# Samples' local attention over all 128 rows: both heads' scores in one matmul, padded values

## The chip, the cores and the metric

One Trainium2 chip, of which the program uses one core. The metric is the device time of one execution in microseconds. The engines are named as in the profile: PE (matrix products), PEld (its weight loads), DVE, ACT, POOL and SP; each works off its own list of instructions in order, and DMAs are issued from SP, ACT and POOL.

## The reference

One step of a streaming encoder of two layers: 512 prompt frames and 8 samples of 16 new frames each, model width 2048. Each layer projects the normalised input with `w_in`, splits the result among three groups (a causal convolution, a sliding-window attention with 16 query heads of 64 over 2 key heads, an attention over 256 memory tokens), gates them, and adds an output projection with `w_out` to the residual. The change touches the window attention of the samples: each sample's 16 frames read 128 cached keys and its own 16.

```python
def swa_sample(q, k, v, cache_k, cache_v, sinks, bias):
    qh = q.reshape(B, S, 2, 8, 64)                   # key heads, queries per key head, width
    kf = jnp.concatenate([cache_k, k], axis=1)       # 128 + 16 keys
    vf = jnp.concatenate([cache_v, v], axis=1)
    o = sink_attention(qh, kf, vf, bias, None, sinks)
    ...
def sink_attention(q, k, v, bias, mask, sinks):
    s = jnp.einsum('...ikgd,...jkd->...kgij', q, k).astype(jnp.float32) * SWA_SCALE + bias
    ...
    p = jnp.exp(s - m)
    w = p / (jnp.sum(p, axis=-1, keepdims=True) + jnp.exp(sink - m))
    return jnp.einsum('...kgij,...jkd->...ikgd', w, v)
```

## The kernel before

Activations are held with channels on the 128 partitions and 640 frames (512 + 8 x 16) in the free dimension. A layer runs 46 projections of `w_in`, each 4 x 4 x 3 x 2 matmuls over 320 columns (`proj`, L749): weights and activations are split in a high and a low part (`wh`, `wl`; `split`, L138 on ACT and L139 on DVE) and three of the four products are taken. Between these matmuls stand those of the attention groups. Their values are plain f32, whose matmul leaves two records in the profile.

The order on each engine is the scheduler's: it places the instructions by a timeline of its own, with priorities, and `issue_after` adds an order between two instructions. Attention work is written as generators with one `yield` between scores and values; `push` starts the next one's first half and then finishes the last one's second half. The samples' generators, `swa_sample(l, b0, held)` for `b0` = 0, 2, 4, 6, are pushed after the last `q` projection and after the following one. Each handles two samples; they are called pairs 1 to 4 in the following.

On the partitions, rows 0 to 63 belong to key head 0 and rows 64 to 127 to key head 1: of the queries `qs` (128 columns a sample: 8 queries by 16 frames) as of the keys `kc` (144 columns a sample: 128 cached, 16 new). The two heads' scores are two matmuls that contract 64 rows each (L571). DVE adds the bias and takes the maximum (L574), ACT takes the exponential (L587), DVE normalises (L600). PE transposes the weights, 128 and 16 columns apart (L603, L604), ACT copies both out of PSUM (L606, L607), and two matmuls into the same sum contract 128 cached values (L608) and 16 new ones (L609).

Of tiles: `kc` has one buffer, `g2` (values, weights, copies, also of the prompt's attention and of the pointwise weights) eight, PSUM's `a` four. POOL loads `kc` (L555) and copies the new keys in (L556), once for pairs 1 and 2 and once for pairs 3 and 4; it also loads the cached values (L558), the new frames' values from a scratch in DRAM (L560), the pointwise weights of the convolution group (L470, used at L477) and the samples' memory keys (L672). Before the samples come the prompt's generators (`swa_prompt`, transposes L528 and L531, values L540), and behind all projections the splits of the gated result into `HL` and its combinations, on DVE and ACT, and the output projection (L749 and L810). L203 sums squares or values over partitions with a matrix of ones, in f32.

Of the kernel before, what the change touches and what calls it, by code (L numbers as in the profile page):

```python
# [12 lines left out]
AF = mybir.ActivationFunctionType  # L13
# [3 lines left out]
P = 128  # L17
# [7 lines left out]
ST = 16  # L25
# [33 lines left out]
def build(nc, tc, ctx, A):  # L59
# [23 lines left out]
    def tl(shape, tag, bufs, dt=F32, pl=None):  # L83
        uid[0] += 1
        pl = pl or (cur[home[tag]] if tag in home else sb)
        return pl.tile(shape, dt, tag=tag, name=f"{tag}_{uid[0]}", bufs=bufs)
# [7 lines left out]
    def g2(shape, dt=F32):  # L94
        return tl(shape, "g2", 8, dt)
# [10 lines left out]
    def pa():  # L106
        return tl([P, 512], "a", 4, F32, ap_)
# [4 lines left out]
    ve, ac, gp, pe, sy = nc.vector, nc.scalar, nc.gpsimd, nc.tensor, nc.sync  # L112
# [6 lines left out]
    ident = sb.tile([P, P], F32, tag="ident", name="ident")  # L119
# [125 lines left out]
    def lsm(l, base, n=1):  # L245
        o = l * SM_L + base
        return sm[:, o:o + n]
# [301 lines left out]

    def swa_sample(l, b0, held):  # L550
        sk = lsm(l, SM_SS, 2)
        if b0 % 4 == 0:
            kc = tl([P, 576], "kc", 1).rearrange("p (b n) -> p b n", b=4)
            with tc.issue_after(late):
                gp.dma_start(kc[:, :, :P], A["ckT"][l, b0:b0 + 4].rearrange("b p n -> p b n"))  # L555
            gp.tensor_copy(kc[:, :, P:], ks[:, b0 * ST:(b0 + 4) * ST].rearrange("p (b n) -> p b n", b=4))  # L556
            vb = g2([P, 4, P])
            gp.dma_start(vb, A["cv"][l, b0:b0 + 4].rearrange("b p n -> p b n"))  # L558
            vn = g2([ST, 4, P])
            gp.dma_start(vn, vscr[l, b0 * ST:(b0 + 4) * ST, :].rearrange("(b i) d -> i b d", i=ST))  # L560
            held[:] = [kc, vb, vn]
        kc, vb, vn = held
        mx, ng, es, sm_, rd = (sml([P, 2, 2]) for _ in range(5))
        xs = []
        for bb in range(2):
            b = b0 + bb
            ps = pa().rearrange("p (j n) -> p j n", j=2)
            x = g2([P, 2, 144])
            for h in range(2):
                rows = slice(h * 64, (h + 1) * 64)  # L570
                pe.matmul(  # L571
                    ps[:, h, :144], qs[rows, b * P:(b + 1) * P], kc[rows, b % 4, :], start=True, stop=True
                )
                ve.tensor_tensor_reduce(  # L574
                    out=x[:, h, :], in0=ps[:, h, :144], in1=bias_s[:, h, :], scale=1.0, scalar=-3.0e38,
                    op0=ALU.add, op1=ALU.max, accum_out=mx[:, bb, h:h + 1],
                )
            xs.append(x)
        skb = sk.unsqueeze(1).to_broadcast([P, 2, 2])
        ve.tensor_tensor(out=ng, in0=mx, in1=skb, op=ALU.max)  # L580
        ve.tensor_scalar(out=ng, in0=ng, scalar1=-1.0, scalar2=None, op0=ALU.mult)
        ve.tensor_tensor(out=es, in0=ng, in1=skb, op=ALU.add)
        ac.activation(es, es, AF.Exp)
        for bb in range(2):
            x = xs[bb]
            for h in range(2):
                ac.activation(  # L587
                    x[:, h, :], x[:, h, :], AF.Exp, bias=ng[:, bb, h:h + 1], accum_out=sm_[:, bb, h:h + 1]
                )
        ve.tensor_tensor(out=es, in0=es, in1=sm_, op=ALU.add)  # L590
        ve.reciprocal(rd, es)
        yield
        pss = [pa(), pa()]
        po = pa().rearrange("p (j n) -> p j n", j=2)
        for bb in range(2):
            x = xs[bb]
            b = b0 + bb
            ps = pss[bb]
            for h in range(2):
                ve.tensor_scalar(  # L600
                    out=x[:, h, :], in0=x[:, h, :], scalar1=rd[:, bb, h:h + 1], scalar2=None, op0=ALU.mult
                )
                pe.transpose(ps[:, h * P:(h + 1) * P], x[:, h, :P], ident)  # L603
                pe.transpose(ps[:ST, 256 + h * P:256 + (h + 1) * P], x[:, h, P:], ident)  # L604
            pt = g2([P, 512])
            ac.activation(pt[:, :256], ps[:, :256], AF.Copy)  # L606
            ac.activation(pt[:ST, 256:], ps[:ST, 256:], AF.Copy)  # L607
            pe.matmul(po[:, bb, :], vb[:, b % 4, :], pt[:, :256], start=True, stop=False)  # L608
            pe.matmul(po[:, bb, :], vn[:ST, b % 4, :], pt[:ST, 256:], start=False, stop=True)  # L609
        for bb in range(2):  # L610
            s, b4 = divmod(b0 + bb, 4)
            for h in range(2):
                rows = slice(h * 64, (h + 1) * 64)
                o = s * HT + PT_ + b4 * ST
                y = R[rows, B0:B0 + 8, o:o + ST]
                ve.tensor_tensor(
                    out=y, in0=po[rows, bb, h * P:(h + 1) * P].rearrange("p (t i) -> p t i", i=ST), in1=y,
                    op=ALU.mult,
                )
# [669 lines left out]
```

## Time and profile before

| | |
|---|---|
| median of 3 runs | 1848.38 us (1848.2 to 1850.27) |
| the profiled execution | 1848.52 us |
| its span, first to last instruction | 1846.7 us |
| mean granted clock of PE | 0.997 |
| PE, PEld busy | 1817.5 us, 1766.3 us |
| DVE, ACT, POOL busy | 1257.8 us, 786.6 us, 160.7 us |
| score matmuls L571 | 64 records, mean 318 ns |
| value matmuls L608, L609 | 32 records each, mean 379 and 426 ns |
| transposes L603, L604 | 32 records each, mean 290 and 272 ns |

An engine's busy time is the union of its instructions' lengths; matmuls are pipelined, so a record's length is longer than what it adds to the engine's time, which shows in the distance from one start to the next. In a timeline row stand the start, the length, engine, line, operation, tiles (written <- read), shape and count of merged records, and in brackets the idle time ahead with what ended it.

### The profile page before, as it was taken

Reading aid. Unit: us, or ns where it says so; the run is one execution under the profiler, and the core shown is the slowest. Engines: PE = TensorE matmul, PEld = TensorE weight load, DVE = VectorE, ACT = ScalarE, POOL = GpSimd, SP = SyncE. Lnnn points to the kernel's source line nnn. Section 1 sums busy time; section 2 is a strip of 40 time slices with the busy share of each in tenths; the row PEclk is TensorE's granted clock in tenths of the full one; section 3 lists DMA queues with packets and bytes.
Section 4 is the critical chain, followed back from the end, with each engine's and each line's share of the span. In section 5 each row is a group of like instructions: output and inputs, shape, how many; then the busy total and the mean of one; then the engine's idle time right before and its main releaser. Section 6 shows DMA issues by size and latency. Waiting matters only on the chain.

```text
span 1846.7 us, 32347 instructions
## 1 busy us (share of the span) xinstructions
PE 1817.5 (98%) x12612; PEld 1766.3 (96%) x12612; DVE 1257.8 (68%) x2562; ACT 786.6 (43%) x1609; POOL 160.7 (9%) x351
## 2 busy tenths in 40 slices
PE   8999999999999999999999999999999999999996
PEld 7999999999998999999999999999999899989996
DVE  7959989567555435966686999766655444676765
ACT  7832224556544334533352222555755333533331
POOL 1121210000000010100020000000000010010000
PEclk9999999999999999999999999999999999999998
DMA  8844442222222343543333332222232244452233
GB/s 281 294 122 107 103 127 76 74 63 72 84 81 76 92 158 117 167 135 112 111 98 92 81 86 77 74 68 76 67 87 81 75 132 132 140 175 76 77 113 120
DMA packets 89001, 202.30 MB, mean 110 GB/s; under 512 B 11872, under 2 KB 16912, under 8 KB 88816
## 3 DMA queue, kind: packets, MB, share of 16 engines
q1 hardware_dynamic: 68848, 139.75, 25.3%
q0 software_dynamic: 17536, 57.60, 10.1%
q10 hardware_dynamic: 2464, 2.88, 0.4%
q8 instruction: 99, 1.62, 0.4%
q14 instruction: 54, 0.44, 0.1%
HBM read 184.84 MB, written 20.33 MB: 111 GB/s over the span
## 4 chain that ended last, share of the span: by engine, by line
PE 94%; DVE 3%; DMA 1%; issue 0%; ACT 0%; DVEq 0%; ACTq 0%
PE z L749 59%; PE a L810 9%; PE z L810 9%; PE z L301 2%; PE a L278 2%; PE a L497 2%; PE a L540 2%; PE a L477 2%; PE z L1134 1%; DVE R L1167 1%; PE a L528 1%; DMA wr<-w_in 1%; PE a L636 1%; PE a L675 1%; PE a L662 1%; PE a L571 1%
## 5 line engine op out<-in xcount | busy, mean ns | idle before, releaser
L749 PE MATMUL z<-HL,wh 128*128 128x320 f32 x4992 | 973.8, 312 | 0.0
L749 PEld LDWEIGHTS z<-HL,wh 128*128 128x128 f32 x4992 | 787.8, 188 | 8.9 <-issue 5.6
L749 PE MATMUL z<-HL,wl 128*128 128x320 f32 x2496 | 584.1, 312 | 1.0 <-DVE wl L139 1.0
L749 PEld LDWEIGHTS z<-HL,wl 128*128 128x128 f32 x2496 | 419.6, 188 | 4.5 <-issue 1.6
L138 ACT ACTIVATE wh<-wr 128x512 fp32r<-128x512 f32 x316 | 198.6, 629 | 467.4 <-PE z L749 383.9
L139 DVE TENSOR_TENSOR wl<-wr,wh 128x512 fp32r<-128x512 f32 x316 | 217.7, 689 | 177.8 <-ACT wh L138 165.4
L425 DVE SCALAR_TENSOR_TENSOR R<-R,sm 128x128 f32<-128x128 f32 (+1 forms) x480 | 235.2, 550 | 0.1
L138 ACT ACTIVATE sh<-sr 128x768 fp32r<-128x768 f32 (+1 forms) x125 | 98.2, 788 | 203.3 <-PE z L810 92.4
L810 PE MATMUL z<-HL,sh 128*128 128x320 f32 x728 | 161.1, 309 | 2.9 <-ACT sh L138 2.9
L139 DVE TENSOR_TENSOR sl<-sr,sh 128x768 fp32r<-128x768 f32 (+1 forms) x125 | 110.0, 882 | 38.7 <-ACT sh L138 38.5
L810 PEld LDWEIGHTS z<-HL,sh 128*128 128x128 f32 x728 | 121.6, 188 | 4.0 <-ACT sh L138 4.0
L810 PE MATMUL z<-HL,sl 128*128 128x320 f32 x364 | 113.6, 312 | 2.3 <-DVE sl L139 2.1
L810 PEld LDWEIGHTS z<-HL,sl 128*128 128x128 f32 x364 | 68.3, 188 | 4.9 <-DVE sl L139 4.9
L810 PE MATMUL a<-th,sh 128*128 128x320 f32 x234 | 72.2, 308 | 0.0
L810 PE MATMUL a<-th,sl 128*128 128x320 f32 x234 | 72.2, 308 | 0.0
L810 PE MATMUL a<-tl,sh 128*128 128x320 f32 x234 | 72.2, 308 | 0.0
L810 PE MATMUL a<-HL,sh 128*128 128x320 f32 x312 | 68.9, 308 | 0.0
L139 DVE TENSOR_TENSOR g<-a,g 128x512 fp32r<-128x512 f32 x80 | 49.6, 634 | 27.1 <-ACT g L138 26.5
L501 DVE CUSTOM_DVE_ANT_0 g<-a,R 128x256 f32<-128x256 f32 (+1 forms) x128 | 46.4, 388 | 23.4 <-PE a L497 20.0
L138 ACT ACTIVATE g<-a 128x512 fp32r<-128x512 f32 x80 | 42.2, 552 | 42.3 <-PE a L531 29.9
L513 ACT ACTIVATE g<-g,sml 128x256 f32<-128x256 f32 (+1 forms) x128 | 59.7, 468 | 0.0
L816 DVE TENSOR_TENSOR R<-a,R 128x320 f32<-128x320 f32 x78 | 37.1, 489 | 25.3 <-PE a L810 24.8
(262 smaller groups left out, 2512.0 us busy)
## 6 DMA issues: line engine op xcount, KB each, us to landing
wr<-w_in SPq DMA_DIRECT2D x304, 256.0 KB, 2.7
sr<-w_out SPq DMA_DIRECT2D x52, 384.0 KB, 3.2
sr<-w_out SPq DMA_DIRECT2D x34, 256.0 KB, 2.6
u<-w_mv SPq DMA_DIRECT2D x16, 512.0 KB, 3.8
u<-cmkT POOLq DMA_DIRECT2D x16, 512.0 KB, 4.3
u<-cmv POOLq DMA_DIRECT2D x16, 512.0 KB, 4.4
u<-w_mk SPq DMA_DIRECT2D x14, 512.0 KB, 4.4
R<-xT SPq DMA_DIRECT2D x16, 320.0 KB, 4.1
```

The source lines that it names most:

```text
L138: a = ac.activation(hi, raw, AF.Copy)
L139: v = ve.tensor_tensor(out=lo, in0=raw, in1=hi.bitcast(F32), op=ALU.subtract)
L278: pe.matmul(ps[ct][:, :256], w[:, ws], mslot(l, k, lo), start=k == 0 and n == 0, stop=k == NK - 1 and n == 2,)
L301: pe.matmul(psv[:, m, :], mslot(l, k, lo)[:, ms], w, start=k == 0 and n == 0, stop=k == NK - 1 and n == 2,)
L425: ve.scalar_tensor_tensor(out=o, in0=x, scalar=w, in1=o, op0=ALU.mult, op1=ALU.add)
L477: pe.matmul(ps[:, :HT], w[:, ws], x[:, k, :], start=n == 0, stop=n == 11)
L497: pe.matmul(ps[:, j, c0:256], q[:, p * P:(p + 1) * P], kk[n][h][:, (p - 1) * P + c0:(p + 1) * P], start=n == 0, stop=n == 1,)
L501: ve.tensor_tensor_reduce(out=x[:, j, c0:], in0=ps[:, j, c0:], in1=bt[:, c0:], scale=1.0, scalar=-3.0e38, op0=ALU.add, op1=ALU.max, accum_ ...
L513: ac.activation(x, x, AF.Exp, bias=ng[:, p:p + 1], accum_out=sm_[:, p:p + 1])
L749: pe.matmul(ps[:, s, :HT], w[:, ws], HL[:, lo * NK + k, s * HT:(s + 1) * HT], start=k == 0 and n == 0, stop=k == NK - 1 and n == 2,)
L810: pe.matmul(out, a[:, k * P:(k + 1) * P], b[:, k, :], start=start and k == 0 and i == 0, stop=stop and k == n - 1 and i == 2, skip_group_c ...
L816: ve.tensor_tensor(out=out, in0=ps, in1=out, op=ALU.add)
```

## The change

`kc` keeps its 576 columns, but these are now 2 samples x 2 heads x 144: head 0's keys stand in rows 0 to 63 of their 144 columns and head 1's in rows 64 to 127 of theirs, and the other halves are set to zero once per layer. One matmul of 128 rows and 288 columns gives both heads' scores of a sample. Since `kc` holds one pair, it is loaded and filled for each of the four pairs, each time in two DMAs of 64 rows and two copies. The new frames' values `vn` become a tile of 128 rows, zero but for the last 16, and the second transpose takes the last 128 of the 144 weights instead of the last 16, so that its result has 128 rows, of which the first 112 meet zeros. ACT copies both transposes at once.

```diff
+        if b0 == 0:
+            kc = tl([P, 576], "kc", 1).rearrange("p (b h n) -> p b h n", b=2, h=2)
+            with tc.issue_after(late):
+                for h in range(2):
+                    gp.memset(kc[rows2[1 - h], :, h, :], 0.0)
+            held[:] = [kc]
+        kc = held[0]
+        for h in range(2):
+            rows = rows2[h]
+            with tc.issue_after(late):
+                gp.dma_start(kc[rows, :, h, :P], A["ckT"][l, b0:b0 + 2, rows, :].rearrange("b p n -> p b n"))
+            gp.tensor_copy(
+                kc[rows, :, h, P:], ks[rows, b0 * ST:(b0 + 2) * ST].rearrange("p (b n) -> p b n", b=2)
+            )
         if b0 % 4 == 0:
-            kc = tl([P, 576], "kc", 1).rearrange("p (b n) -> p b n", b=4)
-            with tc.issue_after(late):
-                gp.dma_start(kc[:, :, :P], A["ckT"][l, b0:b0 + 4].rearrange("b p n -> p b n"))
-            gp.tensor_copy(kc[:, :, P:], ks[:, b0 * ST:(b0 + 4) * ST].rearrange("p (b n) -> p b n", b=4))
...
-            vn = g2([ST, 4, P])
-            gp.dma_start(vn, vscr[l, b0 * ST:(b0 + 4) * ST, :].rearrange("(b i) d -> i b d", i=ST))
+            vn = g2([P, 4, P])
+            gp.memset(vn, 0.0)
+            gp.dma_start(
+                vn[P - ST:], vscr[l, b0 * ST:(b0 + 4) * ST, :].rearrange("(b i) d -> i b d", i=ST)
+            )
...
-            ps = pa().rearrange("p (j n) -> p j n", j=2)
+            ps = pa()[:, :288]
+            pe.matmul(
+                ps, qs[:, b * P:(b + 1) * P], kc[:, bb].rearrange("p h n -> p (h n)"), start=True, stop=True
+            )
             for h in range(2):
-                rows = slice(h * 64, (h + 1) * 64)
-                pe.matmul(
-                    ps[:, h, :144], qs[rows, b * P:(b + 1) * P], kc[rows, b % 4, :], start=True, stop=True
-                )
...
-                pe.transpose(ps[:ST, 256 + h * P:256 + (h + 1) * P], x[:, h, P:], ident)
+                pe.transpose(ps[:, 256 + h * P:256 + (h + 1) * P], x[:, h, ST:], ident)
             pt = g2([P, 512])
-            ac.activation(pt[:, :256], ps[:, :256], AF.Copy)
-            ac.activation(pt[:ST, 256:], ps[:ST, 256:], AF.Copy)
+            ac.activation(pt, ps, AF.Copy)
             pe.matmul(po[:, bb, :], vb[:, b % 4, :], pt[:, :256], start=True, stop=False)
-            pe.matmul(po[:, bb, :], vn[:ST, b % 4, :], pt[:ST, 256:], start=False, stop=True)
+            pe.matmul(po[:, bb, :], vn[:, b % 4, :], pt[:, 256:], start=False, stop=True)
```

The text below the change has other line numbers: the projection matmul L749 is L760 in the changed kernel, the score matmul L571 is L582, the value matmuls L608 and L609 are L619 and L620, the transposes L603 and L604 are L615 and L616. The scheduler also places the work anew: PE, DVE and ACT read otherwise from the first sample of a layer to the start of its output projection, POOL at the loads, SP nowhere.

On PE in layer 0, where pair 2's values end and pair 3's scores begin, the program before has (`z` is the projection's sum, `a` a PSUM tile, `g` the weights and values):

```order
L608 MATMUL a_6375<-g_982_6382,g_926_6107 128x256
L609 MATMUL a_6375<-g_982_6382,g_927_6109 128x256
L603 MATMUL a_6374<-ident,g_953_6180 128x128
L604 MATMUL a_6374<-ident,g_953_6180 16x128
L603 MATMUL a_6374<-ident,g_953_6180 128x128
L604 MATMUL a_6374<-ident,g_953_6180 16x128
L571 MATMUL a_6414<-kc_6402,R 128x144
L571 MATMUL a_6420<-kc_6402,R 128x144
L749 MATMUL z_6965<-HL,wl_6999 128x320 x2
```

and the changed one:

```order
L619 MATMUL a_6378<-g_982_6385,g_926_6111 128x256
L620 MATMUL a_6378<-g_982_6385,g_927_6113 128x256
L615 MATMUL a_6377<-ident,g_953_6186 128x128
L616 MATMUL a_6377<-ident,g_953_6186 128x128
L615 MATMUL a_6377<-ident,g_953_6186 128x128
L616 MATMUL a_6377<-ident,g_953_6186 128x128
L582 MATMUL a_6417<-kc_6104,R 128x288
L582 MATMUL a_6422<-kc_6104,R 128x288
L760 MATMUL z_6964<-HL,wh_6997 128x320 x4
```

The first two rows of scores are one head of two samples before (the other heads' rows follow later), and both heads of both samples now. Pair 2's scores stood like this on PE, among the prompt's last values (L540):

```order
L749 MATMUL z_6802<-HL,wl_6806 128x320
L571 MATMUL a_6173<-kc_6104,R 128x144
L540 MATMUL a_6155<-g_941_6151,vl_2724 128x256
L571 MATMUL a_6179<-kc_6104,R 128x144
L749 MATMUL z_6802<-HL,wl_6806 128x320
```

and stand now like this:

```order
L760 MATMUL z_6801<-HL,wh_6804 128x320 x3
L582 MATMUL a_6180<-kc_6104,R 128x288
L760 MATMUL z_6801<-HL,wh_6804 128x320
L760 MATMUL z_6801<-HL,wl_6805 128x320 x2
L760 MATMUL z_6801<-HL,wh_6804 128x320
L540 MATMUL a_6158<-g_939_6147,vl_2724 128x256
L540 MATMUL a_6158<-g_938_6146,vl_2724 128x256
L540 MATMUL a_6158<-g_939_6147,vl_2724 128x256
L582 MATMUL a_6185<-kc_6104,R 128x288
```

They read keys that were loaded after pair 1's scores, where they had been in `kc` from the start of the layer before. On POOL in layer 0 the loads at this place were, up to the second pointwise weights behind them:

```order
L558 DMA g_926_6107<-cv 128x4x128
L560 DMA g_927_6109<-vscr 16x4x128
L555 DMA kc_6402<-ckT 128x4x128
L556 COPY kc_6402<-R 128x4x16
L470 DMA g_961_6228<-w_pw 128x512
```

and are now:

```order
L562 DMA kc_6104<-ckT 64x2x128
L563 COPY kc_6104<-R 64x2x16
L562 DMA kc_6104<-ckT 64x2x128
L563 COPY kc_6104<-R 64x2x16
L568 DMA g_926_6111<-cv 128x4x128
L570 MEMSET g_927_6113 128x512
L571 DMA g_927_6113<-vscr 16x4x128
L562 DMA kc_6104<-ckT 64x2x128
L563 COPY kc_6104<-R 64x2x16
L562 DMA kc_6104<-ckT 64x2x128
L563 COPY kc_6104<-R 64x2x16
L470 DMA g_961_6231<-w_pw 128x512
```

Pair 2's keys come ahead of the cached values, pair 3's ahead of the pointwise weights; the first pair's keys are loaded early in the layer, as all of pair 1's and 2's were.

More of the change, by code (lines that the diff above doesn't have):

```diff
@@ L551, in swa_sample @@
         sk = lsm(l, SM_SS, 2)
+        if b0 == 0:
[12 more added lines that the diff above has]
+            )
         if b0 % 4 == 0:
-            kc = tl([P, 576], "kc", 1).rearrange("p (b n) -> p b n", b=4)
-            with tc.issue_after(late):
-                gp.dma_start(kc[:, :, :P], A["ckT"][l, b0:b0 + 4].rearrange("b p n -> p b n"))
-            gp.tensor_copy(kc[:, :, P:], ks[:, b0 * ST:(b0 + 4) * ST].rearrange("p (b n) -> p b n", b=4))
             vb = g2([P, 4, P])
             gp.dma_start(vb, A["cv"][l, b0:b0 + 4].rearrange("b p n -> p b n"))
-            vn = g2([ST, 4, P])
-            gp.dma_start(vn, vscr[l, b0 * ST:(b0 + 4) * ST, :].rearrange("(b i) d -> i b d", i=ST))
-            held[:] = [kc, vb, vn]
-        kc, vb, vn = held
+            vn = g2([P, 4, P])
[3 more added lines that the diff above has]
+            )
+            held[1:] = [vb, vn]
+        vb, vn = held[1:]
         mx, ng, es, sm_, rd = (sml([P, 2, 2]) for _ in range(5))
@@ L566, in swa_sample @@
             b = b0 + bb
-            ps = pa().rearrange("p (j n) -> p j n", j=2)
+            ps = pa()[:, :288]
             x = g2([P, 2, 144])
+            pe.matmul(
+                ps, qs[:, b * P:(b + 1) * P], kc[:, bb].rearrange("p h n -> p (h n)"), start=True, stop=True
+            )
             for h in range(2):
-                rows = slice(h * 64, (h + 1) * 64)
-                pe.matmul(
-                    ps[:, h, :144], qs[rows, b * P:(b + 1) * P], kc[rows, b % 4, :], start=True, stop=True
-                )
                 ve.tensor_tensor_reduce(
-                    out=x[:, h, :], in0=ps[:, h, :144], in1=bias_s[:, h, :], scale=1.0, scalar=-3.0e38,
+                    out=x[:, h, :], in0=ps[:, h * 144:(h + 1) * 144], in1=bias_s[:, h, :], scale=1.0, scalar=-3.0e38,
                     op0=ALU.add, op1=ALU.max, accum_out=mx[:, bb, h:h + 1],
```

## The prediction

> **What bounds the kernel now.** I read the page first: the span and engine shares, then the chain that ended last; then the windows over the stretch in which the samples' local attention runs, then its timeline on PE, instruction by instruction.
>
> ```profile
> span 1846.7 us, 32347 instructions
> PE 1817.5 (98%) x12612; PEld 1766.3 (96%) x12612; DVE 1257.8 (68%) x2562; ACT 786.6 (43%) x1609; POOL 160.7 (9%) x351
> PE 94%; DVE 3%; DMA 1%; issue 0%; ACT 0%; DVEq 0%; ACTq 0%
> L749 PEld LDWEIGHTS z<-HL,wh 128*128 128x128 f32 x4992 | 787.8, 188 | 8.9 <-issue 5.6
> ...
> 540.00:640.00 100.00, 100.00 (x656) 90.11 (x654) 52.22 (x154) 41.40 (x117) 7.86 (x15) 1.00 0.29 83
> 1400.00:1500.00 100.00, 100.00 (x656) 90.10 (x655) 51.73 (x153) 41.03 (x118) 7.93 (x15) 1.00 0.27 81
> ```
>
> PE is the chain for 94% of the span. The last two rows are the windows in which layers 0 and 1 do this attention; after the length come PE, PE's weight loads, DVE, ACT and POOL. PE is busy for all 100 us at clock 1.00, DVE for 52, ACT for 41, POOL for 8. So in this stage a microsecond off PE is a microsecond off the end, and the other engines have room. A busy PE need not be a well used one, so I price each product by what it pushes back: the start of a later projection matmul, minus the start of an earlier one, minus 0.147 us for each projection matmul between.
>
> ```profile
> 561.44 0.75 PE L749 MATMUL z<-HL,wh 128*128 128x320 f32 x4
> 562.02 0.46 PE L749 MATMUL z<-HL,wl 128*128 128x320 f32 x2
> 562.32 0.27 PE L603 MATMUL a<-ident,g 128*128 128x128 f32 x1
> 562.42 0.27 PE L604 MATMUL a<-ident,g 128*16 128x128 f32 x1
> ...
> 563.34 0.45 PE L749 MATMUL z<-HL,wl 128*128 128x320 f32 x2
> 563.72 0.76 PE L571 MATMUL a<-kc,R 64*128 64x144 f32 x4
> 564.40 0.86 PE L749 MATMUL z<-HL,wh 128*128 128x320 f32 x4
> 565.10 0.46 PE L749 MATMUL z<-HL,wl 128*128 128x320 f32 x2
> ...
> 571.15 0.46 PE L749 MATMUL z<-HL,wl 128*128 128x320 f32 x2
> 571.44 0.60 PE L608 MATMUL a<-g,g 128*128 128x256 f32 x2
> 571.97 0.69 PE L609 MATMUL a<-g,g 16*128 16x256 f32 x2
> 572.59 0.85 PE L749 MATMUL z<-HL,wh 128*128 128x320 f32 x4
> 573.28 0.46 PE L749 MATMUL z<-HL,wl 128*128 128x320 f32 x2
> ...
> 590.82 0.45 PE L749 MATMUL z<-HL,wh 128*128 128x320 f32 x2
> 591.20 0.51 PE L571 MATMUL a<-kc,R 64*128 64x144 f32 x2
> 591.64 0.56 PE L749 MATMUL z<-HL,wh 128*128 128x320 f32 x2
> 592.03 0.46 PE L749 MATMUL z<-HL,wl 128*128 128x320 f32 x2
> ```
>
> Columns: start, length, engine, line, operation, tiles, shape, count; an f32 matmul leaves two records. The first two rows give the yardstick: six projection matmuls from 561.44 to 562.32, 0.147 each.
> - Two heads' scores side by side: 563.34 to 565.10 is 1.76, less 6 x 0.147 = 0.88 us.
> - One head's scores alone: 590.82 to 592.03 is 1.21, less 4 x 0.147 = 0.62 us. Streaming its 144 columns explains 0.24 of that, if columns cost what they cost in the row of ones below.
> - A sample's two value products: 571.15 to 573.28 is 2.13, less 6 x 0.147 = 1.25 us.
>
> The gap stands where the number of contracted rows changes: 563.34 has two matmuls and yet 0.38 to the next start, and the 128-row product L608 takes 0.53 before the 16-row L609 takes 0.62 for the same 256 columns. What would 128 rows throughout cost? The nearest f32 product of 128 rows among projection matmuls is the sum over tokens at L203, 320 columns:
>
> ```profile
> 405.08 0.75 PE L749 MATMUL z<-HL,wh 128*128 128x320 f32 x4
> 405.66 0.28 PE L540 MATMUL a<-g,vl 128*128 128x256 f32 x1
> 405.78 0.70 PE L203 MATMUL a<-w,ones 128*128 128x320 f32 x2
> 406.07 0.70 PE L749 MATMUL z<-HL,wl 128*128 128x320 f32 x2
> 406.61 0.32 PE L749 MATMUL z<-HL,wh 128*128 128x320 f32 x1
> ```
>
> 405.08 to 406.61 is 1.53, less 6 x 0.147 and 0.12 for L540: 0.53 us, that is 0.00166 per column and nothing left over for a change of rows.
>
> **The change part by part.**
> *Scores.* In a layer the 16 one-head matmuls stand at ten places, the first and last of them quoted: five alone, four in pairs, one group of three from 587.24 to 587.92.
>
> ```profile
> 544.59 0.51 PE L571 MATMUL a<-kc,R 64*128 64x144 f32 x2
> ...
> 587.24 0.76 PE L571 MATMUL a<-kc,R 64*128 64x144 f32 x6
> 587.92 0.41 PE L749 MATMUL z<-HL,wl 128*128 128x320 f32 x1
> ...
> 595.21 0.76 PE L571 MATMUL a<-kc,R 64*128 64x144 f32 x4
> ```
>
> Now 5 x 0.62 + 4 x 0.88 + 0.68 = 7.3 us; then 8 matmuls of 288 columns at 288 x 0.00166 = 0.48, 3.8 us. Saved: 3.5 per layer. Bounds: nothing saved if the 0.38 left over sticks to every f32 product (rival 1), and 3.5 if L203 is the right row; I take L203, the nearest in rows and columns.
> *Values.* Now 8 x 1.25 = 10.0 us; then 16 products of 256 columns over 128 rows at 0.425, 6.8. Saved: 3.2 per layer; nothing, if the second product keeps its 0.72 (a loss would be rival 3).
> *Transposes.* L603, whose result has 128 rows, and L604, whose result has 16, both stream the identity's 128 columns, and follow each other 0.10 apart. Cost of the taller result: none.
> *ACT.* One copy of 512 columns for two of 256: a fixed part saved 16 times, on an engine with 58 us idle in the window. None on the path. DVE keeps its instructions.
> *POOL and its DMAs.* Keys come in halves, four times per layer into the one tile `kc`, instead of twice.
>
> ```profile
> 564.77 0.76 POOL L555 DMA_DIRECT2D kc<-ckT  x1 [17.53 <-PE a L571]
> 565.57 0.24 POOL L556 COPY kc<-R 128x64 f32<-128x64 f32 x1
> ...
> masks.py:197 POOL MEMSET ident<- 128x128 f32 x1 | 0.2, 223 | 0.0
> ...
> DMA to landing us min/median/max: 3.3/5.0/15.2
> ...
> DMA to landing us min/median/max: 3.1/3.4/3.8
> ```
>
> The last two rows are the landings of the key loads (L555) and of the old values (L558). Added per layer: six issues at 0.76 or less, six copies at 0.24, two value memsets (0.22 for 128 columns, so at most 0.9 for 512) and two key memsets of some 0.5: about 9 us of POOL in a layer, under its 92 idle. The first keys of a layer come long before their use. Each reload waits for both score matmuls before it, and behind it on POOL stand the old values, the new frames' values and then the pointwise weights at L470. L470 now follows pair 3's reload, which waits for pair 2's scores: by the counting in rival 2 these end at about 555, against 564.77 where the reload of before began, so the weights are issued earlier, not later. The old values, now behind pair 2's reload, are issued by some 549 and land 4 us later; by the same counting their first product stands after 560. What it costs if this cover fails is rival 2.
> *Order.* The scheduler re-sorts PE, DVE and ACT down to the start of the output projection. There PE does wait now:
>
> ```profile
> 774.74 0.56 PE L749 MATMUL z<-HL,sl 128*128 128x320 f32 x2 [1.66 <-DVE sl L139]
> ...
> PE z L810 <- DVE sl L139: 2.0, 2, 1.5
> PE z L810 <- ACT sh L138: 1.8, 2, 1.4
> ```
>
> The first row is layer 0, the others sum 1625 to 1660 in layer 1: 5.5 us together. The order moves the same DVE and ACT splits past each other here; they may lose all of these waits or double them, so from -5.5 to +5.5, and I take 0, since the same splits still wait for the last projection.
>
> Sum: 2 x (3.5 + 3.2) = 13.4; where transposes follow a value product directly a little of the 1.25 is theirs, so I round to 13. The profiled execution took 1848.5 us, 1.8 more than its span, which I leave as it is; the median of the runs is 1848.4. **1848.5 - 13.0 = 1835.5 us.**
>
> **The rivals.** 0.2% of this time, 3.7 us, is about what a measurement can tell from no change.
> 1. *The left-over belongs to f32, not to the rows.* Then a merged score costs 0.48 + 0.38 = 0.86, 6.9 per layer, and the values stay: 0.4 per layer saved, 1847.7. For it: L608 too has 0.10 more than its 256 columns ask. Against it: L203 shows none.
> 2. *PE waits for reloaded keys* (slower, if late enough). Between pair 1's second score matmul and pair 2's first, the new order has 36 projection matmuls, 7 transposes and 5 products of the prompt: 36 x 0.147 + 7 x 0.11 + 0.46 = 6.5 us; between pair 3 and pair 4 it has 42 and one sample's values, 7.0. The reload needs 0.3 to wake (the scores at 563.72 last to 564.48, the DMA starts at 564.77), 0.76 + 0.24 for the first half, and the second half's landing: at 3.4, 4.7 us. It is hidden with 1.8 to spare. Landings of 5.2 start a stall; at 8.7 the four tight reloads cost 2 x 3.5 + 2 x 3.0 = 13 and eat the gain; at the 15.2 of the slowest landing above, 2 x 10.0 + 2 x 9.5 = 39, 1874. Against it: the four loads of old values, all in this stage, took 3.1 to 3.8. Half-way, at 6.6, 4.6 us are lost: 1840.
> 3. *Weight loads come out from under.* If a 128-row weight load could not run under the matmul before it, each record would show it: 0.188 at the page's `L749 PEld` row, so 0.86 a score, 1.61 a sample's values, 19.8 per layer for 17.3: 1853.5. Against it: projection matmuls start every 0.147 although each loads 128 rows afresh. The Trainium skill (TensorE: Matmul & The Clock Gate, Part 3, The mechanism) says that a weight load overlaps running matmuls only when their row group differs, which is this rival; the trace contradicts it for 128 rows after 128 rows.
> 4. *Height is free, so padding the values saves nothing.* Then only the scores gain: 7.0 us, 1841.5. Against it: L609's 0.62 beside L608's 0.53. The Trainium skill (same page, Why this matters for your kernels) has a matmul of 32 rows taking the time of one of 128; standing next to 128-row work, it does not here.
> 5. *The re-sorted splits wait more*: 5.5 us lost, 1841.
>
> **How the numbers follow.** Forecast 0.66; reloads partly seen 0.07; rival 4 0.07; rival 5 0.08; rival 1 0.07; rival 2 in full 0.03; rival 3 0.02. Range: 1831 (4.5 of the 5.5 us of waits at the output projection vanish) to 1843.5, which takes in the middle cases and leaves out rivals 1, 3 and 2 in full, 0.12, and a little at both edges. Faster (under 1844.7): 0.66 + 0.07 + 0.07 + 0.08 = 0.88; within 0.2%: 0.07; slower: 0.05.
>
> **What would show it.** After: 16 score matmuls of 128 x 288 in two records each, 0.48 us per matmul by the same subtraction; 0.85 for a sample's values, no gap before either; no PE wait for `kc`. PE's matmuls between 540 and 640 would advance by about 6.5 us, and layer 1's by 13. Wrong would be: a wait on PE at the merged score matmul (rival 2), 0.86 there (1 or 3), or PE waits at the output projection that grow by several us (5).

## The result, and the profile after

| | before | after |
|---|---|---|
| median, us | 1848.29 (1846.78 to 1850.27) | 1834.43 (1833.57 to 1836.21) |
| span of the profiled execution, us | 1846.7 | 1831.8 |
| PE records | 12612 | 12580 |

The changed kernel takes 0.9929 of the time before, 95% interval 0.9917 to 0.994: 13.9 us less by the medians. The forecast was 1835.5 with a range of 1831 to 1843.5. The output projection L810 is L821 in the changed kernel, and the key loads L555 are L562.

The page, and the windows of the two layers' local attention, for which the columns are those of before:

```profile
span 1831.8 us, 32312 instructions
PE 1803.6 (98%) x12580; PEld 1766.5 (96%) x12580; DVE 1258.1 (69%) x2562; ACT 785.0 (43%) x1593; POOL 174.0 (9%) x383
...
540.00:640.00 100.00, 100.00 (x681) 96.54 (x680) 55.01 (x158) 42.99 (x112) 13.07 (x27) 1.00 0.31 90
1400.00:1500.00 100.00, 100.00 (x702) 95.96 (x702) 51.12 (x147) 39.30 (x100) 14.97 (x31) 1.00 0.34 100
```

PE is still busy for all 100 us at the full clock. What changed is how much it gets through: 681 records where there were 656, and 702 where there were 656 (the second window begins 8.5 us further on in the program's work than before). PE's weight loads rise from 90 to 96 us with them. The share of busy time, 98%, shows nothing of this.

The timeline on PE around a sample's score matmul, and around a sample's two value products:

```profile
552.84 0.60 PE L760 MATMUL z<-HL,wh 128*128 128x320 f32 x3
553.28 0.65 PE L582 MATMUL a<-kc,R 128*128 128x288 f32 x2
553.55 0.52 PE L760 MATMUL z<-HL,wh 128*128 128x320 f32 x1
553.91 0.46 PE L760 MATMUL z<-HL,wl 128*128 128x320 f32 x2
...
566.95 0.31 PE L760 MATMUL z<-HL,wh 128*128 128x320 f32 x1
567.10 0.59 PE L619 MATMUL a<-g,g 128*128 128x256 f32 x2
567.53 0.59 PE L620 MATMUL a<-g,g 128*128 128x256 f32 x2
567.77 0.79 PE L760 MATMUL z<-HL,wh 128*128 128x320 f32 x3
568.40 0.45 PE L760 MATMUL z<-HL,wl 128*128 128x320 f32 x2
```

The same subtraction as in the prediction: 552.84 to 553.91 is 1.07, less 4 x 0.147 = 0.48 us for both heads' scores. 566.95 to 568.40 is 1.45, less 4 x 0.147 = 0.86 for a sample's values. The next projection matmul now starts under the second record of the product before it (553.55 under the row from 553.28), and both products of values last alike.

The weight loads (PEld), which these timelines leave out, show the difference too. First those at a sample's value products before, then, after the gap, those after:

```profile
571.30 0.34 PEld L608 LDWEIGHTS a<-g,g 128*128 128x128 f32 x2
571.97 0.29 PEld L609 LDWEIGHTS a<-g,g 16*128 16x128 f32 x2 [0.33 <-issue]
572.59 0.59 PEld L749 LDWEIGHTS z<-HL,wh 128*128 128x128 f32 x4 [0.33 <-issue]
```

```profile
567.31 0.41 PEld L620 LDWEIGHTS a<-g,g 128*128 128x128 f32 x2
567.75 0.41 PEld L760 LDWEIGHTS z<-HL,wh 128*128 128x128 f32 x2
```

After the change L620's weights begin to load at 567.31, while the product before it streams, and its matmul starts at 567.53. Before, where the number of rows changed, the load began only together with its own matmul, at 571.97 and again at 572.59, and PEld was idle for 0.33 us ahead of both. From start to start PE then took 0.53, 0.62 and 0.69 us (571.44 to 573.28, in the prediction's rows) where the columns ask for 0.43, 0.43 and 0.59: 0.10 us is lost ahead of the 16-row product, 0.19 at it and 0.10 behind it. What holds the load back the trace does not show.

Where the time went is seen by counting PE's matmuls with the samples' own scores, transposes and values left out (12420 in both kernels) and comparing when the same number starts:

| matmul | before, us | after, us | difference | since the row above |
|---|---|---|---|---|
| 3600, ahead of layer 0's samples | 532.14 | 532.10 | 0.0 | |
| 4500, behind them | 678.40 | 671.92 | -6.5 | -6.4 |
| 5400, in layer 0's output projection | 803.20 | 794.69 | -8.5 | -2.0 |
| 9300, ahead of layer 1's samples | 1366.06 | 1357.57 | -8.5 | 0.0 |
| 11100, behind them | 1632.55 | 1617.35 | -15.2 | -6.7 |
| 12300, near the end | 1817.76 | 1802.33 | -15.4 | -0.2 |

13.1 us come from the two stages, 2.2 from the output projections. A second profiled execution of the changed kernel (`after_again`) gives the same 6.4 and 6.7 us in the stages, but at the output projections it gains 1.8 us in layer 0 and loses 1.6 in layer 1: 0.2 together. So the 13.1 us are what the change gives each time, and what the output projections add differs by 2 us between two executions of one kernel. PE's waits for splits in the first of the two are these (engine, tile and line, what was waited for: us in total, times, longest):

```profile
PE z L760 <- DVE sl L139: 3.7, 2, 2.3
PE z L821 <- ACT sh L138: 1.9, 2, 1.4
PE z L821 <- DVE sl L139: 0.7, 2, 0.4
```

They are the same splits as before, at other places. The same three rows came to 7.1 us before and come to 6.3 now, so they account for only a part of the 2.2. No row names `kc`.

### The profile page after: what moved, and what is told of

Read it like the earlier page. It is cut to its first block, busy times and chain, and to the rows that moved or that the text cites. A ratio compares the mean times of both kernels' runs of the same rounds, so it can differ in the third digit from the quotient of the medians.

```text
span 1831.8 us, 32312 instructions
## 1 busy us (share of the span) xinstructions
PE 1803.6 (98%) x12580; PEld 1766.5 (96%) x12580; DVE 1258.1 (69%) x2562; ACT 785.0 (43%) x1593; POOL 174.0 (9%) x383
## 4 chain that ended last, share of the span: by engine, by line
PE 94%; DVE 3%; DMA 2%; issue 1%; ACT 0%; SPq 0%; DVEq 0%; ACTq 0%; POOLq 0%
PE z L760 59%; PE a L821 9%; PE z L821 9%; PE a L278 2%; PE z L301 2%; PE a L497 2%; PE a L540 2%; PE a L477 2%; PE z L1145 1%; DVE R L1178 1%; PE a L528 1%; DMA wr<-w_in 1%; PE a L647 1%; PE a L673 1%; PE a L686 1%
## 5 line engine op out<-in xcount | busy, mean ns | idle before, releaser
L760 PE MATMUL z<-HL,wh 128*128 128x320 f32 x4992 | 979.5, 312 | 0.0
L760 PEld LDWEIGHTS z<-HL,wh 128*128 128x128 f32 x4992 | 788.9, 188 | 7.9 <-issue 5.3
L760 PE MATMUL z<-HL,wl 128*128 128x320 f32 x2496 | 580.4, 311 | 0.7 <-DVE wl L139 0.7
L760 PEld LDWEIGHTS z<-HL,wl 128*128 128x128 f32 x2496 | 419.3, 188 | 2.0 <-DVE wl L139 1.0
L821 PE MATMUL z<-HL,sh 128*128 128x320 f32 x728 | 160.9, 309 | 1.9 <-ACT sh L138 1.9
L821 PEld LDWEIGHTS z<-HL,sh 128*128 128x128 f32 x728 | 121.7, 188 | 2.4 <-ACT sh L138 2.4
L821 PE MATMUL z<-HL,sl 128*128 128x320 f32 x364 | 113.4, 312 | 0.9 <-DVE sl L139 0.7
L821 PE MATMUL a<-th,sh 128*128 128x320 f32 x234 | 72.2, 308 | 0.0
L821 PE MATMUL a<-tl,sh 128*128 128x320 f32 x234 | 72.2, 308 | 0.0
L821 PE MATMUL a<-th,sl 128*128 128x320 f32 x234 | 72.2, 308 | 0.0
L821 PEld LDWEIGHTS z<-HL,sl 128*128 128x128 f32 x364 | 68.3, 188 | 3.2 <-DVE sl L139 3.2
L821 PE MATMUL a<-HL,sh 128*128 128x320 f32 x312 | 68.9, 308 | 0.0
L485 POOL DMA_DIRECT2D R<-brep x32 | 17.3, 541 | 407.3 <-issue 238.2
```

The costliest lines, as they stand in the source:

```text
L760: pe.matmul(ps[:, s, :HT], w[:, ws], HL[:, lo * NK + k, s * HT:(s + 1) * HT], start=k == 0 and n == 0, stop=k == NK - 1 and n == 2,)
L821: pe.matmul(out, a[:, k * P:(k + 1) * P], b[:, k, :], start=start and k == 0 and i == 0, stop=stop and k == n - 1 and i == 2, skip_group_c ...
```

## The experiments

The theory: the time saved is what PE lost each time it left 128-row work for a matmul of 64 or 16 rows and came back. The rivals: the fewer instructions save, not the rows (merged scores, one copy on ACT); the cost falls gradually with the height; or the scheduler's new order does it. Times below are medians, with the ratio to the kernel before on the same chip and its 95% interval.

**One half of the change at a time.** The score half alone: the changed kernel with 16 rows of new values.

```diff
-            vn = g2([P, 4, P])
-            gp.memset(vn, 0.0)
-            gp.dma_start(vn[P - ST:], ...)
+            vn = g2([ST, 4, P])
+            gp.dma_start(vn, ...)
...
-                pe.transpose(ps[:, 256 + h * P:...], x[:, h, ST:], ident)
-            ac.activation(pt, ps, AF.Copy)
+                pe.transpose(ps[:ST, 256 + h * P:...], x[:, h, P:], ident)
+            ac.activation(pt[:, :256], ps[:, :256], AF.Copy)
+            ac.activation(pt[:ST, 256:], ps[:ST, 256:], AF.Copy)
```

> The changed kernel with its values left as before (16 rows of vn, 16-row second transposes, two ACT copies): the score half of the change alone. Theory (0.4 us per leaving of 128-row work): the scores cost 0.48 us each, 3.5 us less per layer: -6.9 us, 1841.4 us; a sample's values stay at 1.25 us. Rival (the left-over belongs to f32, not to the rows): -0.8 us, 1847.5 us, 0.86 us per score matmul. With the values' half it should add up to the change's 13.9 us; what is missing from the sum is waits.

Measured: 1840.25 us, 0.9959 (0.9945 to 0.9973), 6.8 us less than the 1847.01 before. A lone score costs 0.484, a sample's values 1.25. As the theory had it; the rival that gave the left-over to f32 is out.

The value half alone is the kernel before with the reverse of that diff.

> The kernel before with the value half of the change alone: vn padded with zero rows to 128, second transposes of 128 columns, one ACT copy; the scores stay one head per matmul over 64 rows. Theory (the time saved is what PE loses, about 0.4 us, each time it leaves 128-row work for a 16- or 64-row matmul and comes back): a sample's values fall from 1.25 to 0.86 us, 16 times: -6.3 us, 1842.0 us. Rival A (the height of a matmul is free; only the merging of the scores saves): 0, 1848.3 us. Rival B (all comes from the new order of DVE and ACT splits at the output projection): 0 for the values, and the PE waits at L749/L810 would change by the whole of it.

Measured: 1843.57 us, 0.998 (0.9971 to 0.9989): 3.4 us less, not 6.3. The local price is there: a sample's values before projection matmuls cost 0.86. Three things make up the rest. First, not all 16 samples gained 0.39: where values stand straight ahead of transposes the gain is 0.34, and one sample in each layer stands ahead of 64-row scores, so that PE leaves 128 rows there all the same; it gained 0.20. Over all, the places on PE with samples' scores, transposes and values fell from 51.2 to 45.7 us, by 5.5. Second, counted as above, the same matmuls then lose 0.5 us in each layer at the samples' memory attention, where the re-sorted order has the 32-column products (L704, here L706) in one place more. Third, the output projections give 1.2 us in layer 0 and take 1.2 in layer 1. With 0.4 us by which this execution is ahead at the first sample already, that makes 4.7 us between the two profiled executions; it is 3.4 between the medians. The halves do not add up to 13.9 (6.8 + 3.4 = 10.2). In the two stages they give 6.7 and 5.5 where the whole change gives 13.1, and 0.4 of what is missing there are the two samples that gained only 0.20. The rest goes with the order, which is another in each version, and with the difference from one execution to the next; how much with each is open.

**Merged or not.** The changed kernel with its two heads apart, over 128 rows each:

```diff
-            pe.matmul(ps, qs[...], kc[:, bb].rearrange("p h n -> p (h n)"), start=True, stop=True)
             for h in range(2):
+                pe.matmul(ps[:, h * 144:(h + 1) * 144], qs[...], kc[:, bb, h, :], start=True, stop=True)
```

> The changed kernel with the two heads' scores not merged: two matmuls of 128 rows x 144 columns per sample against the padded keys, in place of one of 288. Theory (the height is what saves): two cost 2 x 0.24 = 0.48 us, as one merged: 1834.4 us, the same as the changed kernel. Rival (fewer matmuls and fewer weight loads are what saves): the score's gain is lost, +6 us, 1840 to 1841 us.

Measured: 1833.51 us, 0.9923 (0.991 to 0.9935), the same as merged. One head's scores in its timeline:

```profile
585.30 0.31 PE L760 MATMUL z<-HL,wl 128*128 128x320 f32 x1
585.44 0.41 PE L583 MATMUL a<-kc,R 128*128 128x144 f32 x2
585.59 0.40 PE L760 MATMUL z<-HL,wl 128*128 128x320 f32 x1
585.83 0.75 PE L760 MATMUL z<-HL,wh 128*128 128x320 f32 x4
```

585.30 to 585.83 is 0.53, less 2 x 0.147 = 0.24 us for 144 columns, where 64 rows cost 0.62 alone. The same number of score matmuls as before the change, at nearly the same places: the rows save, not the merging.

**A height between.** The kernel before with `vn` padded to 64 rows:

```diff
-            vn = g2([ST, 4, P])
+            vn = g2([64, 4, P])
+            gp.memset(vn, 0.0)
...
-                pe.transpose(ps[:ST, ...], x[:, h, P:], ident)
+                pe.transpose(ps[:64, ...], x[:, h, 144 - 64:], ident)
...
```

> The kernel before with vn padded with zero rows to 64, not 128, second transposes of 64 columns, two ACT copies as before. Theory (the loss is paid for a height other than the neighbours' 128, whatever it is): nothing saved, a sample's values stay at 1.25 us: 1848.3 us. Rival (the cost falls as the rows rise, or a memset tile or wider transposes save by themselves): between, -2 to -4 us, 1844 to 1846 us.

Measured: 1847.27 us, 0.9998 (0.999 to 1.0007). A memset tile, taller transposes and 64 rows save nothing that the time shows:

```profile
570.84 0.46 PE L752 MATMUL z<-HL,wl 128*128 128x320 f32 x2
571.13 0.60 PE L611 MATMUL a<-g,g 128*128 128x256 f32 x2
571.66 0.70 PE L612 MATMUL a<-g,g 64*128 64x256 f32 x2
572.28 0.85 PE L752 MATMUL z<-HL,wh 128*128 128x320 f32 x4
572.97 0.46 PE L752 MATMUL z<-HL,wl 128*128 128x320 f32 x2
```

570.84 to 572.97 is 2.13, less 6 x 0.147 = 1.25, the same as for 16 rows, at four times their height. At one place in each layer the trace does show a gain: where three 64-row scores follow a sample's values and so a product of their own height, all of them cost 1.50 us instead of 1.94. That fits the theory, in which it is the neighbours' height that counts.

**One leaving for two products.** The kernel before with a pair's two 128-row products first and its two 16-row ones side by side. In it the two samples' sums stand open in one PSUM tile at the same time, and what it leaves there are other values than before; instructions and shapes are those of before.

```diff
+        for bb in range(2):
+            last_vb = pe.matmul(po[:, bb, :], vb[...], pts[bb][:, :256], start=True, stop=False, ...).ins
+        with tc.issue_after(last_vb):
+            for bb in range(2):
+                pe.matmul(po[:, bb, :], vn[:ST, ...], pts[bb][:ST, 256:], start=False, stop=True, ...)
```

> The kernel before with the order inside a pair's value products changed: both samples' 128-row products first, then both 16-row products, which stand next to each other on PE. The work is the same. Theory (about 0.35 us are lost each time PE leaves 128-row work and comes back, whatever it does meanwhile): one leaving per pair in place of two, 8 of 16 saved, -2.7 us on PE: 1844 to 1845.5 us, and a pair's two 16-row products cost one surplus. Rival (the surplus belongs to each 16-row product): no change in their cost, 1847 to 1848 us.

Measured: 1848.73 us, 1.0008 (0.9999 to 1.0016): no gain. But where a pair's four products stand together, the local price is the theory's:

```profile
599.10 0.45 PE L760 MATMUL z<-HL,wh 128*128 128x320 f32 x2
599.39 0.59 PE L612 MATMUL a<-g,g 128*128 128x256 f32 x2
599.91 1.12 PE L617 MATMUL a<-g,g 16*128 16x256 f32 x4
600.97 0.56 PE L760 MATMUL z<-HL,wh 128*128 128x320 f32 x2
601.36 0.46 PE L760 MATMUL z<-HL,wl 128*128 128x320 f32 x2
```

599.10 to 601.36 is 2.26, less 4 x 0.147 = 1.68 for one 128-row and two 16-row products; with the other 128-row product, 0.43 at its place, a pair costs 2.11 instead of 2.50 (2.46 where one of its samples stands ahead of transposes). The second 16-row product costs 0.43, its 256 columns and nothing more. So the 0.39 belongs to the leaving. That holds for two of a layer's four pairs. In the other two the order put another product between the pair's two 128-row products (a score; in the last pair one of the memory attention, of 32 columns), and there the scores, the values and what stands between cost as much as before or 0.2 more. So the places on PE with scores, transposes and values fell from 51.2 to 50.3 us only, and counted as above PE is no further ahead at layer 0's output projection than before. The whole time could not show it; the timeline could.

**A leaving by itself, and its control.** The changed kernel with one more matmul of 16 columns behind each score, over 16 rows and over 128:

```diff
-            ps = pa()[:, :288]
+            full = pa()
+            ps = full[:, :288]
...
+            pe.matmul(full[:, 496:512], qs[:16, ...], kc[:16, bb, 0, :16], start=True, stop=True)   # or [:128]
```

> The changed kernel with one more matmul behind each sample's score matmul, 16 rows by 16 columns, into unused columns of the same PSUM tile; nothing reads it. Theory (the loss is that of leaving 128-row work, not of the matmul's own size): 0.35 to 0.4 us for each of 16, +5.6 to +6.4 us: 1839 to 1841 us. Rival (a matmul costs by its columns, 0.00166 us each, and a little per record): at most 0.1 us each, 1834 to 1836 us.

> The control for the 16-row one: the same 16 more matmuls of 16 columns, but over 128 rows. Theory and rival alike: by columns 16 x 0.00166 = 0.03 us, with two records at their shortest spacing up to 0.12 us: +0.5 to +2 us, 1834 to 1836.5 us. If this one too costs 0.35 us each, it is any additional matmul and not the height that costs, and the theory falls.

Measured: 16 rows 1840.59 us, 0.9956 (0.9943 to 0.997); 128 rows 1835.27, 0.9931 (0.9918 to 0.9943). First the one over 16 rows, then, after the gap, the one over 128:

```profile
552.75 0.46 PE L764 MATMUL z<-HL,wh 128*128 128x320 f32 x2
553.05 0.65 PE L583 MATMUL a<-kc,R 128*128 128x288 f32 x2
553.62 0.39 PE L586 MATMUL a<-kc,R 16*128 16x16 f32 x2
553.95 0.41 PE L764 MATMUL z<-HL,wl 128*128 128x320 f32 x1
554.20 0.52 PE L540 MATMUL a<-g,vl 128*128 128x256 f32 x3
```

```profile
553.03 0.45 PE L764 MATMUL z<-HL,wh 128*128 128x320 f32 x2
553.32 0.65 PE L583 MATMUL a<-kc,R 128*128 128x288 f32 x2
553.81 0.29 PE L586 MATMUL a<-kc,R 128*128 128x16 f32 x2
553.95 0.39 PE L764 MATMUL z<-HL,wl 128*128 128x320 f32 x1
554.17 0.51 PE L540 MATMUL a<-g,vl 128*128 128x256 f32 x3
```

1.45 - 3 x 0.147 - 0.48 = 0.53 us for the 16-row one, 1.14 - 3 x 0.147 - 0.48 = 0.22 for the 128-row one. The matmul with an eighth of the rows costs 0.3 us more, 16 times 4.9 of the 5.3 us between the two medians. The control's 0.22 is more than the 0.12 expected: on PEld the weight loads around it, 0.19 us long, start 0.11 us apart (553.81, 553.92, 554.03), and 16 columns are over sooner than that (0.03 us by the price per column), so two records cost two such distances. The changed kernel's products are longer and cost what their columns ask. At the 16-row one the loads again start only with their own matmuls, at 553.62 and, back at 128 rows, at 553.94.

**Both halves of the rows at once.** The changed kernel with 64-row scores again, heads alternating, each in its own PSUM tile:

```diff
+        for bb in range(2):
+            for h in range(2):
+                with tc.issue_after(prev) if prev else nullcontext():
+                    prev = pe.matmul(pht[h][:, bb * 144:...], qs[rows2[h], ...], kc[rows2[h], bb, h, :], ...).ins
...
```

> The changed kernel with its values padded as they are, but the scores again one head per matmul over that head's 64 rows, a pair's four in the order head 0, head 1, head 0, head 1, each head in a PSUM tile of its own. On PE they stand as one and three at pairs 1, 2 and 4, as four in a row at pair 3. Theory (leaving 128-row work costs about 0.4 us once, and matmuls on the two halves of the rows run at the same time, as two of them start 13 ns apart in the trace of before): 0.62 for the one, 0.68 for the three, 2 x 0.24 + 0.4 = 0.88 for the four; 4.8 us per layer against 3.9 for eight merged: +1.8 us, 1836 us. Rival (halves do not overlap): 0.62, 3 x 0.24 + 0.4 = 1.12 and 1.36, 6.6 us per layer: +5.4 us, 1840 us.

Measured: 1839.09 us, 0.9951 (0.9937 to 0.9965): between the two, and nearer to the rival's 1840. The timeline decides. The group of three at pair 4:

```profile
587.70 0.31 PE L765 MATMUL z<-HL,wh 128*128 128x320 f32 x1
587.93 0.75 PE L584 MATMUL a<-kc,R 64*128 64x144 f32 x6
588.62 0.57 PE L765 MATMUL z<-HL,wh 128*128 128x320 f32 x2
589.02 0.27 PE L620 MATMUL a<-ident,g 128*128 128x128 f32 x1
```

587.70 to 589.02 is 1.32, less 3 x 0.147 = 0.88 for three. The one ahead of it costs 0.63 by the same counting, and pair 3's four in a row 0.89 (2.19 for a group with a sample's values and transposes, less 0.86 and 0.44): no more than three, and no more than two of the same half before the change. So the halves do overlap. The three were expected at 0.68, the price of before's group of three, but that one stood behind a 16-row product: on its way from 128 rows to 16, to 64 and back PE changes three times instead of four. With 0.88 a layer's scores cost 3 x (0.63 + 0.88) + 0.89 = 5.4 against 3.9 merged, 3 us for both layers; the median stands some 4 to 5 above the changed kernel.

The Trainium skill (TensorEngine Tiling (Array Packing), Tiling Modes, Key Properties) says that a change of tiling mode drains the engine and that tiles of one mode run independently. The trace fits both, though it shows no drain as such: 0.39 us a leaving, and two halves that start 7 ns apart. Here two samples' four products packed cost 0.89, padded 0.97, and only if all four stand together.

**Late keys.** The changed kernel with twelve memsets of the rows that are zero anyway at each reload:

```diff
+        if b0:
+            for _ in range(6):
+                for h in range(2):
+                    gp.memset(kc[rows2[1 - h], :, h, :], 0.0)
```

> The changed kernel with each reload of the keys held up: twelve further memsets of the rows that are zero anyway (0.35 us each in the trace of the changed kernel, 4.2 us together) stand on POOL ahead of pairs 2, 3 and 4's first key load. The trace of the changed kernel has 1.5 us to spare at pair 2. Theory (the order is made with POOL's work in it, and PE has other work): the pair's scores are only put some 38 matmuls later on PE, PE waits for no keys, 1834 to 1836 us. Rival (a late reload stalls PE, as in the prediction's second rival): 2.7 us at pair 2 of each layer and up to as much at pairs 3 and 4, +5 to +14 us: 1840 to 1848 us, with PE waits for kc.

Measured: 1833.8 us, 0.9921 (0.9907 to 0.9935), the same as without. Pair 2's reload in the trace of the changed kernel, and its landing times:

```profile
547.12 0.62 POOL L562 DMA_DIRECT2D kc<-ckT  x1 [15.54 <-PE z L760]
...
548.37 0.60 POOL L562 DMA_DIRECT2D kc<-ckT  x1
...
DMA to landing us min/median/max: 3.4/3.4/3.4
```

The second half is there at 548.37 + 3.4 = 551.77, the score matmul starts at 553.28: 1.5 us to spare. With the memsets:

```profile
551.86 2.27 POOL L562 MEMSET kc<- 64x288 f32 x6
...
558.02 1.13 PE L586 MATMUL a<-kc,R 128*128 128x288 f32 x4
```

The last memset ends at 554.13, 2.4 us later than the keys had been there; the order, made with these memsets in it, puts the scores at 558.02, behind 38 more matmuls, and PE waits for nothing. The memsets slipped in between and behind the loads (the first load starts at 546.95), so the loads themselves were not late, other than was expected; what came late were the last rows of the tile. A landing that comes late without the scheduler's knowing, which is what the prediction's second rival needs, wasn't tried.

**A further version.** If PE's cost goes by columns at one height, the half of each value product that is thrown away (each head's columns for the other head's queries) is worth cutting. Old values lie per head with zeros in the other head's columns; head 1's new frames stand ahead of its old ones, so that one window of 128 columns holds both heads' new frames:

```diff
+        vb = g2([P, 2, 2, P])        # sample, head; the other head's columns zero
...
+                pe.transpose(ps[:, h * P:(h + 1) * P], xf[:, h * 160:h * 160 + P], ident)
+            pe.transpose(ps[:, 256:384], xf[:, 32:160], ident)
+            for h in range(2):
+                pe.matmul(po[:, bb, :], vb[:, bb, h, :], pt[:, h * P:(h + 1) * P], start=h == 0, stop=False)
+            pe.matmul(po[:, bb, :], vn[:, b % 4, :], pt[:, 256:], start=False, stop=True)
...
```

> A further version: the old values lie per head with the other head's columns zero, head 1's new frames stand ahead of its old ones, so that one transpose of 128 columns holds both heads' new frames, and a sample's values are three products of 128 x 128 into one 128 x 128 tile in place of two of 128 x 256; three transposes in place of four, and one multiply for both heads. Theory (at one height PE's cost goes by columns alone): 128 columns less at 0.00166 us, 0.21 us, and a transpose less, 0.11 us, 16 times: -5.1 us, 1829.3 us. Rival (more matmuls and weight loads per column cost something, or the two more memsets and loads on the way of the values make PE wait): 1832 to 1836 us.

> The changed kernel itself once more, on the same chip and beside the same runs of the kernel before as the next one, so that the two can be compared: 0.993 of the kernel before.

> The version with the old values per head and three products of 128 columns, beside the changed kernel on the same chip. Theory: PE's cost by columns and transposes, 0.673 for a sample's values and 0.31 for its transposes against 0.86 and 0.44: 16 x 0.32 = 5.1 us less than the changed kernel, 0.990 of the kernel before. Rival (the first comparison's 0.9885 against 0.9929 is all real): 8 us less, 0.9885.

Measured: 1827.1 us, 0.9885 (0.9872 to 0.9899); a second time 1827.64, 0.9886 (0.9873 to 0.99), beside the changed kernel's 1834.77, 0.992 (0.9906 to 0.9933). It beats both kernels; 7.1 us less than the changed one where 5.1 were expected. A sample's values:

```profile
566.68 0.46 PE L766 MATMUL z<-HL,wh 128*128 128x320 f32 x2
566.97 0.61 PE L628 MATMUL a<-g,g 128*128 128x128 f32 x4
567.41 0.39 PE L629 MATMUL a<-g,g 128*128 128x128 f32 x2
567.56 0.55 PE L766 MATMUL z<-HL,wh 128*128 128x320 f32 x2
567.94 0.46 PE L766 MATMUL z<-HL,wl 128*128 128x320 f32 x2
```

566.68 to 567.94 is 1.26, less 4 x 0.147 = 0.67, with three weight loads in place of two; three transposes cost 0.31 for 0.44. That is 0.32 us, 16 times. Counted as above, the two stages give 4.6 and 4.7 us more than the changed kernel's in the two profiled executions of this version. The other 2 us lie at the output projections, where these two executions gain 2.1 and 3.1 us on the kernel before and the changed kernel's two gained 2.2 and 0.2; what makes them differ is open, and single executions of this version alone differ by 3 us (1825.07 to 1828.09).

## Why the prediction was right, point by point

- *What bounds the stage.* Right: a microsecond off PE came off the end, while POOL's share of the windows rose from 8 to 13 and 15 us at no cost.
- *The price at one height.* Right, 0.48 expected and 0.48 found for a score, 0.85 and 0.86 for the values. L203, a product in another place of the kernel with the same number of rows, gave it.
- *Scores.* 7.0 us for both layers; alone they gave 6.8.
- *Values.* 6.4 us for both layers; alone, 5.5 at their places on PE and 3.4 in the whole. The term was a little too large by itself (a sample ahead of transposes gains 0.34), and it took for granted that 64-row scores behind it would be gone too, which in the whole change they are. In the whole change both terms together gave 13.1 where 13.4 was summed.
- *The group of three.* Its 0.68 held only where it stood, behind a 16-row product, which had paid for the leaving: behind 128-row work three cost 0.88, 0.20 more, which is half of 0.39 for one change of rows more. In the sum that does no harm, since both products go, but it is why the value half alone gained 0.20 there and not 0.39.
- *Order: 0, within 5.5 either way.* It was 2.2 us less in one profiled execution and 0.2 less in the other, and nothing that the change had to bring: with the value half alone the two projections give 1.2 and take 1.2. Added to the 13.1 it gives the 15.4 by which the first profiled execution is shorter; the medians differ by 13.9. That the forecast lies within 1.1 us of the median is thus partly luck, since it depends on how this term falls. The 5.5 also left out waits of 1.4 us at the same two places (0.68 and 0.17 in layer 0, for example), so it was not the whole of what could be lost or doubled.
- *Transposes, ACT, POOL at nothing.* Right; no wait for them appeared.
- *The rivals.* Rival 1 is refuted by the score half alone. Rival 2 did not occur: 1.5 us to spare at pair 2, where 1.8 was worked out. Rival 3, by the Trainium skill (TensorE: Matmul & The Clock Gate, Part 3, The mechanism), would have had weight loads come out from under; the same section also lets a load run ahead into a background weight buffer. With 128 rows behind 128 rows none came out, except at products of 16 columns. It was at a change of rows, in the kernel before, that a load did not run ahead. Rival 4, by the same page of the Trainium skill (Why this matters for your kernels), held for the streaming, 0.43 for 256 columns of either height, but not for the neighbours: 0.39 more at a change of rows. Rival 5 had the sign wrong in both profiled executions.

## What to carry to other kernels

Where PE is the bound and works through one shape, a small matmul of fewer rows can cost as much by its switch as by its work or more (0.39 us beside 0.43 for 256 columns, 0.38 beside 0.24 for 144): look in the timeline for gaps at a change of the row count, and pad to the neighbours' height, all the way, since half-way saved nothing among 128-row work. If padding isn't possible, let the small ones stand together. After that the columns are what is left to cut, and a half of an output that is thrown away is the first place to look; and an edit of 0.2% in a scheduled kernel is read in the timeline at its place, since the re-sorting around it, and one execution against the next, are worth 1 to 2 us here.

## What the runs showed of the hardware

- Leaving 128-row work and coming back costs 0.39 us around products of 256 columns over 16 or 64 rows, and 0.3 around 16 columns, the control taken off. One change of rows fewer on the way saved 0.20, half of it, and at each change the weight load starts only together with its own matmul.
- Two f32 matmuls over the two halves of the rows start 7 to 13 ns apart and share their time: four of 144 columns cost 0.89 us, as three do.
- Weight loads of 128 rows, 0.188 us long, start as little as 0.11 us apart. A product of 144 columns, 0.12 us a record, shows nothing of them; one of 16 columns costs 0.22 us for its two records.
- POOL's memset of 128 x 512 f32 took 0.53 us, one of 64 x 288 0.35.
